# Scores at full height, out projections token-major, and x on a queue of its own, in a two-layer hybrid trunk

## The chip, the core and the metric

The kernel runs on one core of one Trainium2 chip. The metric is the device time of one execution in microseconds (us); the median of three executions of the kernel before is 894.36 us (894.18 to 894.96). One engine multiplies matrices (PE in the profile, with its weight loads as PEld), and beside it work VectorE (DVE), ScalarE (ACT), GpSimd (POOL) and SyncE (SP), each through its own queue of instructions in the order in which the program lists them. DMA transfers are issued from SP, ACT and POOL.

## The reference, cut to what matters

Two layers, a differential attention and a gated linear attention (GLA), over 256 tokens of width 2048, all in float32:

```python
def reference(x, ...):                       # x [1, 256, 2048]
    for i in range(2):
        h = _rmsnorm(x, norm_g[i])           # over the 2048 features
        y = _diff_attention(h, ...) if i == 0 else _gla(h, ...)
        x = x + y
    return x

def _diff_attention(h, w_in, qk_g, lam_vecs, subln_g, w_out, rel_bias, layer_idx):
    q, k, v, g = jnp.split(h @ w_in, 4, axis=-1)       # 16 heads, two halves t of 64 each
    q = _rmsnorm(q.reshape(B, S, H, 2, d), qk_g[0]) * (d ** -0.5)
    k = _rmsnorm(k.reshape(B, S, H, 2, d), qk_g[1])
...
    s = jnp.einsum('bqhtd,bkhtd->bthqk', qblk, k) + bias   # blocks of 128 queries
    s = jnp.where(_chunk_mask(qpos, kpos), s, NEG_INF)     # queries 0..127 see keys 0..127 alone
    p = jax.nn.softmax(s, axis=-1)
    attn = p[:, 0] - lam * p[:, 1]
...
    return (o * jax.nn.silu(g)) @ w_out

def _gla(h, w_in, w_gate, gate_bias, out_g, w_out):
    q, k, v, g, lr = jnp.split(h @ w_in, ...)
...
    return (o * jax.nn.silu(g)) @ w_out
```

## The kernel before, in words

**Products in split float32.** A float32 operand is split exactly into a high and a low part of type float32r ("fp32r" in the rows), and a product is made of three: high by high, low by high, high by low. Weights come in 288 chunks of 512 KB (`weights`, L93 to L110): SP issues the load into `raw` (four buffers, L104), ACT copies the high part (`hi`, L105), DVE subtracts it (`lo`, L108). For the first eight chunks SP also loads a piece of x ahead of the weights (L103), and `prep_x` makes the parts of x times the norm's gain in `aT` (`split_x`: ACT L188, DVE L189).

**Projections.** `project` (L141) takes the next 512 columns token-major, 16 contraction tiles of 128 rows: for each tile and each half t of the tokens three products of 512 columns (L159 to L161) into one bank of `pj` per half, 96 products in all; or it takes 256 columns feature-major: for each tile and each 128 output features one product of 512 columns (the tokens' high and low parts side by side, L163) and one of 256 (L165), 64 in all. The input projections of layer 0 and the values and gates of layer 1 are token-major; both out projections (`for blk in range(8)`) and the keys and queries of layer 1 are feature-major.

**Layer 0.** x lies feature-major in `xT`. Its squares are summed feature by feature: ACT squares (L180), POOL adds them up in `acc` (L182, L184), and `token_scale` (L203) lets PE sum over the partitions with products of one column (`ps_r`, L208). `norm_qk` writes a head's query parts as [high; low] over the 128 rows and the key's high part twice, so that one full-height product (L329) takes two of the three partial products; the third, high query by low key (`kl`), has 64 rows (L333). Each head does this for two halves t and two query blocks, 256 keys wide each, although block 0 uses only its first 128 columns (L339). Transpositions (`pt_qk`, `pt_a`, `pt_y`) are float32 products with the identity. The out projection adds its two halves into `xT` on DVE (L461), splits the sum for layer 1 at once and adds up its squares.

**Order.** The program names engines, not places: a scheduler orders each engine's instructions when the kernel is built. `background` holds generators (attention, gates, GLA) of which `pump` puts a piece behind every few chunks.

## Time and profile before

| | before |
|---|---|
| median of 3 executions | 894.36 us |
| the profiled execution, first to last instruction | 894.6 us |
| PE busy | 881.3 us, 99% |
| DVE, ACT, POOL busy | 573.4, 469.1, 117.9 us |
| mean granted clock of PE | 0.995 |
| DMA | 162.36 MB, mean 181 GB/s |

A busy PE is a row of overlapping products: each row of a product lasts longer than the time until the next one starts, so what a product costs is read from start to start. The rows further down are of four views: the page's first part (busy time, share and count of each engine), the waits, the timeline (start, duration, engine, line, what is written from what, count, and the idle time before), and tables of stretches or of groups of instructions.

### The profile page before, as it was taken

What the parts mean: (1) busy time and instruction counts of PE and PEld (TensorE: products, weight loads), DVE (VectorE), ACT (ScalarE), POOL (GpSimd) and SP (SyncE); (2) the same over time, 40 slices, a digit from 0 to 9 for tenths busy, and PEclk for the clock granted to TensorE, in tenths of its full rate; (3) what the DMA queues carried; (4) which work ended last, traced back from release to release, by engine and by line L of the source; (5) the groups of instructions that cost most, each with busy time, mean ns of one, the idle gap of its engine ahead of it and who ended that gap; (6) DMA issues with size and microseconds to landing.
All of it is one profiled execution on the core that took longest, in us unless ns stands there. A gap on an engine that the chain in (4) does not pass through costs nothing.

```text
span 894.6 us, 11955 instructions
## 1 busy us (share of the span) xinstructions
PE 881.3 (99%) x4388; PEld 733.7 (82%) x4388; DVE 573.4 (64%) x880; ACT 469.1 (52%) x727; POOL 117.9 (13%) x154
## 2 busy tenths in 40 slices
PE   7899999999999999999999999999999999999998
PEld 4688888888878878888888888888888888888886
DVE  5776576677668667565777758945555556555553
ACT  6556566656656655544544448643444444444331
POOL 5421012122012210100411121310000000000000
PEclk9899999999999999999999999999999999999999
DMA  7775555556555554555655545555465556656761
GB/s 268 240 226 183 181 171 186 186 176 198 179 161 169 170 158 150 175 183 183 206 186 190 188 146 176 173 191 172 159 181 172 178 175 186 183 180 194 223 213 46
DMA packets 47995, 162.36 MB, mean 181 GB/s; under 512 B 6048, under 2 KB 8624, under 8 KB 47936
## 3 DMA queue, kind: packets, MB, share of 16 engines
q1 hardware_dynamic: 43200, 153.11, 54.1%
q0 software_dynamic: 2288, 6.38, 2.4%
q10 hardware_dynamic: 2448, 2.11, 0.7%
q8 instruction: 34, 0.56, 0.3%
q14 instruction: 25, 0.20, 0.1%
HBM read 159.46 MB, written 5.27 MB: 184 GB/s over the span
## 4 chain that ended last, share of the span: by engine, by line
PE 96%; DVE 1%; DMA 1%; issue 1%; SPq 0%; ACT 0%; DVEq 0%
PE pj L163 20%; PE pj L159 19%; PE pj L161 19%; PE pj L160 19%; PE pj L165 10%; PE ps_s L329 1%; PE ps_s L333 1%; DMA raw<-in_aw 1%; PE ps_o L614 1%; PE ps_at L600 1%; PE pt_qk L298 1%; PE pt_y L410 1%; PE pt_a L363 1%; DVE aT L189 1%; PE ps_lr L511 0%
## 5 line engine op out<-in xcount | busy, mean ns | idle before, releaser
L108 DVE TENSOR_TENSOR lo<-raw,hi 128x1024 fp32r<-128x1024 f32 (+1 forms) x290 | 354.0, 1222 | 215.8 <-ACT hi L105 212.4
L105 ACT ACTIVATE hi<-raw 128x1024 fp32r<-128x1024 f32 (+1 forms) x290 | 304.8, 1052 | 316.4 <-PE pj L160 169.5
L159 PE MATMUL pj<-hi,aT 128*128 128x512 f32 x768 | 304.8, 397 | 2.2 <-ACT hi L105 2.2
L161 PE MATMUL pj<-lo,aT 128*128 128x512 f32 x768 | 300.5, 394 | 5.3 <-DVE lo L108 5.2
L160 PE MATMUL pj<-hi,aT 128*128 128x512 f32 x768 | 301.9, 393 | 0.5 <-DVE aT L189 0.5
L163 PE MATMUL pj<-y,hi 128*128 128x512 f32 x512 | 179.8, 397 | 0.0
L161 PEld LDWEIGHTS pj<-lo,aT 128*128 128x128 f32 x768 | 144.4, 189 | 37.1 <-DVE lo L108 7.0
L159 PEld LDWEIGHTS pj<-hi,aT 128*128 128x128 f32 x768 | 144.9, 189 | 34.3 <-ACT hi L105 3.5
L160 PEld LDWEIGHTS pj<-hi,aT 128*128 128x128 f32 x768 | 145.0, 189 | 29.4 <-DVE aT L189 0.9
L165 PE MATMUL pj<-y,lo 128*128 128x256 f32 x512 | 143.0, 280 | 0.0
L163 PEld LDWEIGHTS pj<-y,hi 128*128 128x128 f32 x512 | 96.1, 188 | 23.0
L165 PEld LDWEIGHTS pj<-y,lo 128*128 128x128 f32 x512 | 96.4, 188 | 0.2
L163 PE MATMUL pj<-aT,hi 128*128 128x512 f32 x256 | 90.5, 398 | 0.0
L165 PE MATMUL pj<-aT,lo 128*128 128x256 f32 x256 | 71.9, 281 | 0.0
L163 PEld LDWEIGHTS pj<-aT,hi 128*128 128x128 f32 x256 | 48.1, 188 | 11.5
L165 PEld LDWEIGHTS pj<-aT,lo 128*128 128x128 f32 x256 | 48.3, 189 | 0.0
L200 POOL TENSOR_TENSOR rq<-ms,mhalf 128x8 f32<-128x8 f32 x16 | 29.7, 1864 | 24.8 <-DVE ms L288 24.8
L184 POOL TENSOR_TENSOR acc<-acc,sq 128x512 f32<-128x512 f32 x14 | 20.8, 1482 | 67.0 <-ACT sq L180 66.8
L189 DVE SCALAR_TENSOR_TENSOR aT<-xT,ng_sb,aT 128x256 fp32r<-128x256 f32 x32 | 27.9, 906 | 2.6 <-ACT aT L188 2.6
L634 POOL TENSOR_TENSOR kq<-kq,rb 128x256 f32<-128x256 f32 x16 | 17.5, 1099 | 67.5 <-DVE kq L632 62.3
L337 DVE CUSTOM_DVE_ANT_0 s<-ps_s,tb 128x256 f32<-128x256 f32 x32 | 13.5, 422 | 19.1 <-PE ps_s L333 19.1
L320 POOL DMA_DIRECT2D tb<-skew_d x16 | 9.1, 572 | 124.9 <-DVE nm L339 85.3
(166 smaller groups left out, 633.8 us busy)
## 6 DMA issues: line engine op xcount, KB each, us to landing
raw<-in_aw SPq DMA_DIRECT2D x126, 512.0 KB, 3.6
raw<-in_bwvg SPq DMA_DIRECT2D x64, 512.0 KB, 3.5
raw<-in_awo SPq DMA_DIRECT2D x32, 512.0 KB, 4.4
raw<-in_bwkq SPq DMA_DIRECT2D x32, 512.0 KB, 4.1
raw<-in_bwo SPq DMA_DIRECT2D x32, 512.0 KB, 4.4
skew_d<-bias_d POOLq DMA_DIRECT2D x8, 384.0 KB, 5.6
tb<-skew_d POOLq DMA_DIRECT2D x16, 128.0 KB, 2.8
out_dram<-ot ACTq DMA_DIRECT2D x16, 128.0 KB, 4.2
```

What stands on the lines that cost most here:

```text
L105: nc.scalar.activation(hi[:, ks, :], raw[:, ks, :], AF.Copy)
L108: nc.vector.tensor_tensor(out=lo[:, ks, :], in0=raw[:, ks, :], in1=hi[:, ks, :].bitcast(F32), op=ALU.subtract)
L159: nc.tensor.matmul(banks[t], lhsT=xh, rhs=hi[:, kk, :], start=first, stop=False)
L160: nc.tensor.matmul(banks[t], lhsT=xl, rhs=hi[:, kk, :], start=False, stop=False)
L161: nc.tensor.matmul(banks[t], lhsT=xh, rhs=lo[:, kk, :], start=False, stop=last)
L163: nc.tensor.matmul(banks[t], lhsT=hi[:, kk, sl], rhs=lhs[k].rearrange("p a s -> p (a s)"), start=first, stop=False, skip_group_check=True)
L165: nc.tensor.matmul(banks[t][:, 0:S], lhsT=lo[:, kk, sl], rhs=lhs[k][:, 0, :], start=False, stop=last, skip_group_check=True)
L184: nc.gpsimd.tensor_tensor(out=acc, in0=acc, in1=sq, op=ALU.add)
L189: nc.vector.scalar_tensor_tensor(out=dst[k][:, 1, :], in0=xT[:, k, :], scalar=g, in1=dst[k][:, 0, :].bitcast(F32), op0=ALU.mult, op1=ALU.s ...
L200: nc.gpsimd.tensor_tensor(out=dst, in0=src, in1=mhalf[:, 0:n], op=ALU.pow)
L337: nc.vector.tensor_tensor_reduce(out=s[:, t, 0:256], in0=ps[:, 0:256], in1=tb, scale=1.0, scalar=BIG, op0=ALU.add, op1=ALU.min, accum_out= ...
L634: nc.gpsimd.tensor_tensor(out=dst, in0=dst, in1=rb, op=ALU.mult)
```

## The change

1. **Scores.** `kl` is two standing tiles with a half for each t, whose other 64 rows POOL sets to zero at the start. The third partial product becomes a full-height one with the same weights as the first. Query block 0 takes only keys 0 to 127, so that half of a head's eight products are 128 columns wide. The order is now by block, then by t.
2. **Out projections.** Both run token-major, four blocks of 512 columns. The residual x lies token-major in `xk`, loaded from a second copy of x (`xs`) by four SP transfers in the first projection block. DVE adds one bank at a time. The squares are taken token-major by ACT with an accumulated sum (`ssq`), no longer by POOL and PE. For layer 1, PE transposes the new x (`pt_x`, 32 transpositions in 8 groups), and ACT and DVE split it from PSUM.
3. **The start.** The feature-major x comes in five pieces, issued by ACT; DVE instead of ACT copies the high part of the first chunk. The last out block ends its last chunk bank by bank, and its output leaves in halves on two queues.

```diff
-                nc.sync.dma_start(xT[:, kx, :], xt[:, kx, :])
-            nc.sync.dma_start(raw[:, ks, :], src[:, ks, :])
-            nc.scalar.activation(hi[:, ks, :], raw[:, ks, :], AF.Copy)
+                high_x(pos[0] * CK + k, step)
+            if pos[0] == 0:
+                nc.vector.tensor_copy(out=hi[:, ks, :], in_=raw[:, ks, :])
+            else:
+                nc.scalar.activation(hi[:, ks, :], raw[:, ks, :], AF.Copy)
             if pos[0] < NCK:
-                prep_x(pos[0] * CK + k, step)
+                low_x(pos[0] * CK + k, step)
...
+            if tail and c == n - 1:
+                for t in range(2):
+                    for kk in range(ck):
+                        xh, xl = (lhs[c * ck + kk][:, i, t * P:(t + 1) * P] for i in range(2))
...
-    acc = const.tile([P, 2, S], F32, name="acc")
-    def square_sum(src, pool, first):
-        sq = pool.tile([P, 2, S], F32, tag="sq", name="sq", bufs=2 if pool is ta else 1)
-        nc.scalar.activation(sq, src, AF.Square)
-        if first:
-            nc.gpsimd.tensor_copy(acc, sq)
-        else:
-            nc.gpsimd.tensor_tensor(out=acc, in0=acc, in1=sq, op=ALU.add)
-    def split_x(layer, dst, k):
-        g = ng_sb[:, layer, k:k + 1]
-        nc.scalar.activation(dst[k][:, 0, :], xT[:, k, :], AF.Copy, scale=g)
-        nc.vector.scalar_tensor_tensor(out=dst[k][:, 1, :], in0=xT[:, k, :], scalar=g,
-                                       in1=dst[k][:, 0, :].bitcast(F32), op0=ALU.mult, op1=ALU.subtract)
+    xT = big.tile([P, KT, S], F32, tag="y1", name="xT")
+    for a, b in ((0, 1), (1, 2), (2, 4), (4, 8), (8, 16)):
+        nc.scalar.dma_start(xT[:, a:b, :], xt[:, a:b, :])
+    def high_x(k, n):
+        for i in range(k, k + n):
+            nc.scalar.activation(aT[i][:, 0, :], xT[:, i, :], AF.Copy, scale=ng_sb[:, 0, i:i + 1])
+    def low_x(k, n):
+        for i in range(k, k + n):
+            nc.vector.scalar_tensor_tensor(out=aT[i][:, 1, :], in0=xT[:, i, :], scalar=ng_sb[:, 0, i:i + 1],
+                                           in1=aT[i][:, 0, :].bitcast(F32), op0=ALU.mult, op1=ALU.subtract)
+    ssq = const.tile([P, 2, 4], F32, name="ssq")
+    def square_sum(blk, pool):
+        for t in range(2):
+            jk = pool.tile([P, NB], F32, tag="sq", name="sq", bufs=2 if pool is ta else 1)
+            nc.scalar.activation(jk, xk[:, t, blk * NB:(blk + 1) * NB], AF.Square, accum_out=ssq[:, t, blk:blk + 1])
...
-        tot = acc[:, 0, :]
-        nc.vector.tensor_tensor(out=tot, in0=acc[:, 0, :], in1=acc[:, 1, :], op=ALU.add)
-        ps = bank(ptr, "ps_r")
-        for t in range(2):
-            nc.tensor.matmul(ps[:, t:t + 1], lhsT=tot[:, t * P:(t + 1) * P], rhs=ones[:, 0:1],
-                             start=True, stop=True)
         ms = small.tile([P, 2], F32, tag="ms2", name="ms2")
-        nc.vector.tensor_scalar(out=ms, in0=ps[:, 0:2], scalar1=1.0 / D, scalar2=EPS, op0=ALU.mult, op1=ALU.add)
+        nc.vector.tensor_reduce(out=ms, in_=ssq, axis=AX.X, op=ALU.add)
+        nc.vector.tensor_scalar(out=ms, in0=ms, scalar1=1.0 / D, scalar2=EPS, op0=ALU.mult, op1=ALU.add)
...
+    kls = []
+    for i in range(2):
+        kl = ta.tile([P, 2, 4, S], F32R, name=f"kl{i}", bufs=1)
+        for t in range(2):
+            nc.gpsimd.memset(kl[64 - t * 64:128 - t * 64, t].bitcast(F32), 0.0)
+        kls.append(kl)
+    def load_x(c):
         if c >= NCK // 2:
-            for i in (2 * c - NCK, 2 * c - NCK + 1):
-                square_sum(xT[:, i * CK:(i + 1) * CK, :], ta, i == 0)
+            blk = c - NCK // 2
+            cols = slice(blk * NB, (blk + 1) * NB)
+            nc.sync.dma_start(xk[:, :, cols], xs[:, :, cols])
...
-                    nc.vector.tensor_tensor(out=kl[own, :, toks], in0=ptv[own], in1=dst[own].bitcast(F32),
+                    nc.vector.tensor_tensor(out=kl[own, u, :, toks], in0=ptv[own], in1=dst[own].bitcast(F32),
...
-            for qb, c0 in ((1, 0), (0, 256)):
-                qs = [qk[:, t * 4 + h, qb * P:(qb + 1) * P] for t in range(2)]
+            for qb, c0, n in ((1, 0, 256), (0, 256, 128)):
                 for t in range(2):
-                    nc.tensor.matmul(pss[t][:, c0:c0 + S], lhsT=qs[t], rhs=qk[:, 8 + t * 4 + h, :],
+                    q = qk[:, t * 4 + h, qb * P:(qb + 1) * P]
+                    nc.tensor.matmul(pss[t][:, c0:c0 + n], lhsT=q, rhs=qk[:, 8 + t * 4 + h, 0:n],
                                      start=True, stop=False)
-                for t in range(2):
-                    rows = slice(t * 64, (t + 1) * 64)
-                    nc.tensor.matmul(pss[t][:, c0:c0 + S], lhsT=qs[t][rows], rhs=kl[rows, h, :],
-                                     start=False, stop=True)
+                    nc.tensor.matmul(pss[t][:, c0:c0 + n], lhsT=q, rhs=kl[:, t, h, 0:n], start=False, stop=True)
...
-        b = project(aT, True, steps=4 if hg else 0, before=sum_x if hg == 0 else None)
+        b = project(aT, True, steps=4 if hg else 0, before=load_x if hg == 0 else None)
         if hg == 0:
+            for i in range(4):
+                square_sum(i, ta)
+            r1, r1h = token_scale("r1")
             setup_a()
-            r1, r1h = token_scale("r1")
         qk = big.tile([P, KT, S], F32R, tag="y0" if hg % 2 == 0 else "y1", name="qk")
-        kl = ta.tile([P, 4, S], F32R, tag="kl", name="kl")
+        kl = kls[hg % 2]
...
-    for blk in range(8):
-        b = project(yT, False)
-        for j in range(2):
-            k = blk * 2 + j
-            for i in range(2):
-                nc.vector.tensor_tensor(out=xT[:, k, :], in0=b[j][:, i * S:(i + 1) * S], in1=xT[:, k, :], op=ALU.add)
-            split_x(1, bT, k)
-        square_sum(xT[:, blk * 2:blk * 2 + 2, :], tb_, blk == 0)
-    r2, r2h = token_scale("r2")
+    def transpose_x(blk):
+        square_sum(blk, tb_)
+        yield
+        for half in range(2):
+            pt = bank(ptr, "pt_x")
+            for j in range(2):
+                k = blk * 4 + half * 2 + j
+                for t in range(2):
+                    nc.tensor.transpose(pt[:, (j * 2 + t) * P:(j * 2 + t + 1) * P], xk[:, t, k * P:(k + 1) * P], ident)
+            for j in range(2):
+                k = blk * 4 + half * 2 + j
+                g = ng_sb[:, 1, k:k + 1]
+                p = pt[:, j * S:(j + 1) * S]
+                nc.scalar.activation(bT[k][:, 0, :], p, AF.Copy, scale=g)
+                nc.vector.scalar_tensor_tensor(out=bT[k][:, 1, :], in0=p, scalar=g,
+                                               in1=bT[k][:, 0, :].bitcast(F32), op0=ALU.mult, op1=ALU.subtract)
+            yield
+    for blk in range(4):
+        b = project(yT, True, steps=4)
+        cols = slice(blk * NB, (blk + 1) * NB)
+        for t in range(2):
+            nc.vector.tensor_tensor(out=xk[:, t, cols], in0=b[t], in1=xk[:, t, cols], op=ALU.add)
+        background.append(transpose_x(blk))
...
-    background.append(first())
     for h in range(BH):
-        b = project(bT, False, steps=3)
+        b = project(bT, False, steps=3 if h else 0, before=None if h else lambda c: pump((0, 2, 1, 0)[c]))
         if h == 0:
-            drain()
+            r2, r2h = scale_row()
...
-    for blk in range(8):
-        b = project(zT, False)
-        for j in range(2):
-            k = blk * 2 + j
-            ot = gp.tile([P, S], F32, tag="th", name="ot")
-            nc.vector.tensor_tensor(out=ot, in0=b[j][:, 0:S], in1=xT[:, k, :], op=ALU.add)
-            nc.vector.tensor_tensor(out=ot, in0=b[j][:, S:2 * S], in1=ot, op=ALU.add)
-            nc.scalar.dma_start(out[:, k, :], ot)
+    for blk in range(4):
+        b = project(zT, True, tail=blk == 3)
+        for t in range(2):
+            ot = gp.tile([P, NB], F32, tag="th", name="ot")
+            for half in range(2 if blk == 3 else 1):
+                n = NB // 2 if blk == 3 else NB
+                part = slice(half * n, (half + 1) * n)
+                cols = slice(blk * NB + half * n, blk * NB + (half + 1) * n)
+                nc.vector.tensor_tensor(out=ot[:, part], in0=b[t][:, part], in1=xk[:, t, cols], op=ALU.add)
+                (nc.sync if half else nc.scalar).dma_start(out[:, t, cols], ot[:, part])
...
-        "awo": blocks(a["a_w_out"][0], S),
+        "awo": blocks(a["a_w_out"][0], NB),
```

How this moves instructions is shown at two places, the start and the scores. ACT's queue at the start, the kernel before, from the first gains on; `aT` is the scaled x, `sq` the squares, `hi` the high parts of weights:

```order
L188 ACTIVATE aT<-xT,ng_sb 128x256 x2
L180 ACTIVATE sq<-xT 128x512
L105 ACTIVATE hi<-raw 128x1024
L188 ACTIVATE aT<-xT,ng_sb 128x256 x2
L180 ACTIVATE sq<-xT 128x512
L188 ACTIVATE aT<-xT,ng_sb 128x256 x2
L180 ACTIVATE sq<-xT 128x512
L105 ACTIVATE hi<-raw 128x1024
L188 ACTIVATE aT<-xT,ng_sb 128x256 x2
L180 ACTIVATE sq<-xT 128x512
L105 ACTIVATE hi<-raw 128x1024 x6
```

The same queue in the changed kernel, where `xk` is the token-major x:

```order
L108 ACTIVATE hi<-raw 128x1024
L196 ACTIVATE aT<-xT,ng_sb 128x256 x4
L108 ACTIVATE hi<-raw 128x1024
L196 ACTIVATE aT<-xT,ng_sb 128x256 x8
L108 ACTIVATE hi<-raw 128x1024
L209 ACTIVATE sq,ssq<-xk 128x512 x5
L273 ACTIVATE nb<-ps_b 16x384
L209 ACTIVATE sq,ssq<-xk 128x512 x3
L108 ACTIVATE hi<-raw 128x1024
L285 ACTIVATE le<-ls 128x2
L108 ACTIVATE hi<-raw 128x1024 x5
```

All eight squares now stand between the high parts of the fifth and the sixth chunk of weights, and they read `xk`. SP's queue at the start, the kernel before, where `raw` are the weights:

```order
L103 DMA xT<-in_xt 128x512 x2
L104 DMA raw<-in_aw 128x1024
L103 DMA xT<-in_xt 128x512
L104 DMA raw<-in_aw 128x1024 x122
L104 DMA raw<-in_awo 128x1024 x32
```

The same queue in the changed kernel:

```order
L102 DMA raw<-in_aw 128x512 x4
L102 DMA raw<-in_aw 128x1024 x3
L249 DMA xk<-in_xs 128x2x512 x4
L102 DMA raw<-in_aw 128x1024 x123
L102 DMA raw<-in_awo 128x1024 x32
```

The four loads of `xk` stand behind five chunks of weights (the first two in halves) and ahead of the sixth. PE's queue around the scores of a head, the kernel before:

```order
L161 MATMUL pj<-lo,aT 128x512
L329 MATMUL ps_s<-qk 128x256 x2
L333 MATMUL ps_s<-kl,qk 128x256 x2
L329 MATMUL ps_s<-qk 128x256 x2
L333 MATMUL ps_s<-kl,qk 128x256 x2
```

The same place in the changed kernel:

```order
L349 MATMUL ps_s<-qk 128x256
L351 MATMUL ps_s<-kl_120,qk 128x256
L349 MATMUL ps_s<-qk 128x256
L351 MATMUL ps_s<-kl_120,qk 128x256
L349 MATMUL ps_s<-qk 128x128
L351 MATMUL ps_s<-kl_120,qk 128x128
L349 MATMUL ps_s<-qk 128x128
L351 MATMUL ps_s<-kl_120,qk 128x128
```

The eight products of a head still stand together between two products of the projection; where pairs over two t took turns, now each L349 is followed by the L351 of the same t.

## Rows read from the trace of the kernel before

**Rows 1.** The page's first part: busy time, share and count of PE.

```profile
PE 881.3 (99%) x4388; PEld 733.7 (82%) x4388; DVE 573.4 (64%) x880; ACT 469.1 (52%) x727; POOL 117.9 (13%) x154
```

**Rows 2.** The waits of PE, whole program: total us, times, longest.

```profile
PE pj L161 <- DVE lo L108: 5.2, 3, 3.7
PE pj L159 <- ACT hi L105: 2.2, 3, 1.0
```

**Rows 3.** Timeline of PE around the scores of one head: start, duration, what.

```profile
92.49 0.40 PE L329 MATMUL ps_s<-qk 128*128 128x256 f32 x2
92.81 0.38 PE L333 MATMUL ps_s<-kl,qk 64*128 64x256 f32 x2
93.12 0.50 PE L329 MATMUL ps_s<-qk 128*128 128x256 f32 x2
93.56 0.38 PE L333 MATMUL ps_s<-kl,qk 64*128 64x256 f32 x2
...
94.67 0.40 PE L159 MATMUL pj<-hi,aT 128*128 128x512 f32 x1
```

**Rows 4.** Timeline of PE, token-major projection, from one product to the third after it.

```profile
410.00 0.39 PE L161 MATMUL pj<-lo,aT 128*128 128x512 f32 x1
...
410.68 0.39 PE L161 MATMUL pj<-lo,aT 128*128 128x512 f32 x1
```

**Rows 5.** Timeline of PE: four float32r products of full height, 256 columns.

```profile
534.44 0.63 PE L535 MATMUL ps_z<-lrs,wgs 128*128 128x256 f32 x4
534.91 0.28 PE L165 MATMUL pj<-aT,lo 128*128 128x256 f32 x1
```

**Rows 6.** Timeline of PE: float32 products of 128 columns, two passes each.

```profile
135.81 0.39 PE L372 MATMUL po<-v,atT 128*128 128x128 f32 x2
136.04 0.39 PE L373 MATMUL po<-v,atT 128*128 128x128 f32 x2
```

**Rows 7.** Timeline of PE, feature-major out projections: twelve pairs, then thirty-one.

```profile
441.07 0.40 PE L163 MATMUL pj<-y,hi 128*128 128x512 f32 x1
...
445.31 0.40 PE L163 MATMUL pj<-y,hi 128*128 128x512 f32 x1
...
879.20 0.39 PE L163 MATMUL pj<-y,hi 128*128 128x512 f32 x1
...
889.94 0.40 PE L163 MATMUL pj<-y,hi 128*128 128x512 f32 x1
```

**Rows 8.** Timeline of PE around a group of four transpositions.

```profile
403.83 0.60 PE L410 MATMUL pt_y<-ident,th 128*128 128x128 f32 x4
...
404.97 0.40 PE L159 MATMUL pj<-hi,aT 128*128 128x512 f32 x1
```

**Rows 9.** The chain of waits, the one-column products of a token scale.

```profile
520.96 0.34 PE ps_r L208 x4
```

**Rows 10.** Stretches: us, PE, PEld, DVE, ACT, POOL busy (count), PE clock, DMA share, GB/s.

```profile
5.10:27.30 22.20, 17.93 (x68) 11.74 (x66) 16.79 (x23) 16.48 (x32) 11.06 (x12) 1.00 0.81 277
27.30:31.40 4.10, 0.43 (x3) 0.04 (x1) 4.10 (x5) 2.57 (x3) 2.11 (x2) 0.80 0.60 203
31.40:37.00 5.60, 5.60 (x14) 4.42 (x15) 4.43 (x6) 0.77 (x1) 1.77 (x4) 0.54 0.74 212
37.00:41.20 4.20, 4.20 (x21) 3.46 (x20) 2.00 (x2) 1.35 (x2) 0.00 (x0) 1.00 0.99 366
```

**Rows 11.** ACT by form: count, busy us, mean ns; first two of 0:41.2.

```profile
L105 ACT ACTIVATE hi<-raw 128x1024 fp32r<-128x1024 f32 x9 | 9.2, 1049 | 8.5 <-DMA raw<-in_aw 8.4
L188 ACT ACTIVATE aT<-xT,ng_sb 128x256 fp32r<-128x256 f32 x16 | 7.4, 498 | 0.7 <-DMA ng_sb<-in_ng 0.5 <-DMA xT<-in_xt 0.2
...
L617 ACT ACTIVATE jkb<-ps_o 128x512 f32<-128x512 f32 x8 | 4.7, 588 | 2.3 <-PE ps_o L614 2.3
...
L617 ACT ACTIVATION_READ_ACCUMULATOR jkb<-ps_o 128x1 f32 x8 | 1.5, 192 | 0.0
```

**Rows 12.** Timeline of DVE: the last instructions of the program.

```profile
890.83 0.75 DVE L680 TENSOR_TENSOR ot<-pj,ot 128x256 f32<-128x256 f32 x2
```

More of the change, by code (lines that the diff above doesn't have):

```diff
@@ L80, in trunk_kernel @@
         nc.tensor.matmul(idle, lhsT=zero[:, 0:P], rhs=zero, start=True, stop=True)
-    xT = big.tile([P, KT, S], F32, name="xT")
+    xk = big.tile([P, 2, D], F32, name="xk")
     def operand(tags):
@@ L139, in drain, with project @@
             pump()
-    def project(lhs, token_major, steps=0, before=None):
+    def project(lhs, token_major, steps=0, before=None, tail=False):
         banks = [bank(pj, "pj"), bank(pj, "pj")]
@@ L166, in project @@
                                          start=False, stop=last, skip_group_check=True)
+            if tail and c == n - 1:
+                for t in range(2):
+                    for kk in range(ck):
+                        xh, xl = (lhs[c * ck + kk][:, i, t * P:(t + 1) * P] for i in range(2))
+                        nc.tensor.matmul(banks[t], lhsT=xh, rhs=hi[:, kk, :], start=False, stop=False)
+                        nc.tensor.matmul(banks[t], lhsT=xl, rhs=hi[:, kk, :], start=False, stop=False)
+                        nc.tensor.matmul(banks[t], lhsT=xh, rhs=lo[:, kk, :], start=False, stop=kk == ck - 1)
             want = (c + 1) * steps // n
@@ L220, in trunk_kernel @@
     ta = lay_a.enter_context(tc.tile_pool(name="ta", bufs=2))
-    def prep_x(k, n):
-        for i in range(k, k + n):
-            split_x(0, aT, i)
-    def sum_x(c):
+    kls = []
[5 more added lines that the diff above has]
+    def load_x(c):
         if c >= NCK // 2:
-            for i in (2 * c - NCK, 2 * c - NCK + 1):
-                square_sum(xT[:, i * CK:(i + 1) * CK, :], ta, i == 0)
+            blk = c - NCK // 2
+            cols = slice(blk * NB, (blk + 1) * NB)
+            nc.sync.dma_start(xk[:, :, cols], xs[:, :, cols])
     relb_sb = const.tile([32, AH], F32, name="relb_sb")
```

16 lines of the change are left out of this document (9 added, 7 removed).

## The prediction

> **What bounds the kernel now.** The first part of the page shows PE busy for 99% of the span [rows 1]. Read alone, that says only that products overlap, so the waits come next: over the whole program PE waits 5.2 us for low parts of weights and 2.2 us for high parts, three times each [rows 2], and by the timeline all of it lies in the first 32 us. Behind the start PE waits for nothing, so each microsecond taken from PE's row there shortens the program, and nothing done for DVE, ACT or POOL does, as long as none of them becomes late. Durations in PE's rows overlap; I read prices from start to start.
>
> **The change part by part.** The sum is made against the profiled execution's 894.6 us.
>
> *Scores.* The eight products of a head start at 92.49, and the fourth projection product behind them starts at 94.67 [rows 3]. Between lie 2.18 us, less three projection products of 0.227 (three take 0.68 [rows 4]): a head costs 1.50 us. The eight products have 256 columns each, and full-height float32r products of 256 columns, each with weights of its own, run at 0.47 us for four, 0.1175 apiece [rows 5]; eight would be 0.94. The missing 0.56 us is the turn between full and half height: the two half-height products at 92.81 hand over only at 93.12, and the next full-height pair at 93.12 takes 0.44 until 93.56 [rows 3]. The change makes all eight full height, with the same rows of queries as weights. Four keep 256 columns. The other four have 128, and no float32r product of 128 columns is in this trace. From below: half of 0.1175, if columns alone count, 0.059. From above: a float32 product of 128 columns, which is run as two passes, takes 0.23 (135.81 to 136.04 [rows 6]). I take 0.1175, no gain from fewer columns, since the weights are as large as before and rows 5 is the nearest in type. So a head costs 0.94, and 16 heads save 16 x 0.56 = 9.0 us. With 0.059 a head costs 0.71 and the saving is 12.7; with 0.23 it costs 1.39 and the saving is 1.8.
>
> A rule of the Trainium skill speaks against this edit: page "TensorEngine Tiling (Array Packing)", section "Theoretical Speedup", gives up to twofold speed for a contraction of 64 rows or fewer. By it a pair of half-height products would cost one full one, a head before would be 0.71 us, and the edit would lose 0.23 x 16 = 3.8 us. The measured 1.50 of rows 3 leaves that no chance; the same page says that a change of tiling mode drains the engine, which fits the late turns. On width, page "TensorE: Matmul & The Clock Gate", section "Back-to-back issue gap", gives N / 2.4 + 2.5 ns, some 56 ns at 128 columns; no run here shows it yet.
>
> *Out projections.* Columns are the same: per contraction tile and 512 features, four pairs of 512 and 256 before, six products of 512 after. The pace is not. Twelve pairs take 4.24 us in the first out projection, 0.353 a pair, and thirty-one take 10.74 in the second, 0.3465 [rows 7]; 256 pairs each make 90.4 + 88.7 = 179.1 us. Token-major, 256 groups of three at 0.68 [rows 4] make 174.1: 5.0 us saved. From the other side, if token-major took the slower column pace of rows 7, 256 x 0.7066 = 180.9, a loss of 1.8; I take 5.0, since rows 4 are the same instructions on the same shapes. Weights still come in chunks of 512 KB with one ACT copy and one DVE subtraction each, so their supply per product of PE does not change.
>
> *Transpositions of x.* They are new on PE. A group of four starts at 403.83, and the fourth product behind it at 404.97: 1.14 - 0.68 = 0.46 us [rows 8]. Eight groups cost 3.7, and one is torn in two by the order, about 0.1 more: 3.8 us. ACT and DVE split x from PSUM beside PE; the last block's groups stand behind the first products of layer 1, which need them only for the last quarter of their contraction.
>
> *Token scale.* Four records of one column, 0.34 us in the chain [rows 9], go in each layer; with some 0.05 for the turn, 0.8 us saved.
>
> *The start.* Of the first 41 us, 22.2 from 5.1 on hold only 17.9 of overlapping products, then PE stands for 4.1, and from 31.4 to 37.0 it runs at a granted clock of 0.54 [rows 10], near the lower of its two levels of 1.2 and 2.4 GHz, after having stood. 5.6 x (1 - 0.54) = 2.6 us is the price of that. DVE was at work in all of the 4.1 us: its splits of x ran beside POOL's additions. Counted along the timeline, the first block's 96 products are out at 41.2; unhindered from 5.1 on they would be at 26.9. The change takes POOL's additions away but moves the squares: ACT's queue holds eight of them between the high parts of chunks five and six, and they read `xk`, which SP loads behind five chunks of weights. Queued behind them on ACT is every later high part, and PE waits for that. Bytes first: x 2.1 MB, five chunks 2.6, xk 2.1, together 6.8 MB; at 277 GB/s [rows 10] that is 24.5 us from about 2.5 on, so 27; at 366 GB/s, 21. Then ACT: the last piece of x is in at some 16.5 (4.2 MB at 300, between those two rates; ACT's five issues ahead lie within that time), eight gains of 0.46 (they overlap a little; 0.498 each [rows 11]) to 20.2, the high part of chunk five 1.05 to 21.3, eight squares of 0.588 + 0.192 [rows 11] and a small copy of 0.5 to 28.0, the sixth high part to 29.1. PE is done with chunk five at 24.0 and stands for five microseconds, longer than before, so I charge the 2.6 us of the clock again. Three chunks of 36 products, 8.2 us, end at 37.4, with the clock at 40.0: 1.2 us saved. At best, with a fast xk and no fall of the clock, 36: 5 saved. At worst xk comes at 203 GB/s, the lowest rate in rows 10: 6.8 MB take 33.5, two squares and the high part follow at 38.6, then 8.2 + 2.6 make 49.4: 8.2 lost.
>
> That x has a queue of its own I count at nothing: with one queue the DMA engines already reached a share of 0.81 to 0.99 [rows 10].
>
> *The end.* The last two additions of 0.75 us [rows 12] become one second addition of about 0.36, and the halves leave on two queues: 0.4 us saved.
>
> *At nothing:* the zeros of `kl` on POOL lie ahead of all scores; larger squares with an accumulated sum cost ACT time that it has (52% busy [rows 1]); the shift of the phase in which the feature-major products of layer 1 run (0.353 or 0.3465 a pair, 256 pairs) may give or take 1.7 us.
>
> **The sum.** -9.0 - 5.0 + 3.8 - 0.8 - 1.2 - 0.4 = -12.6, so 882.0 us as profiled. The profiled execution lies 0.24 above the median; the forecast for the median is 881.8.
>
> **The rivals.**
> A. *Narrow products are slow.* A float32r product of 128 columns takes the two passes of rows 6, 0.23. For it: those are the only products of that width. Against it: they are float32, not float32r. Scores then save 1.8, and the time is 889.0.
> B. *Only columns count.* 0.059 for 128 columns: 12.7 saved, 878.1. For it: 256 columns of rows 5 cost about half of 512 in rows 4. Against it: the load of 128 columns of weights under each product, which does not shrink. The gap cited above would give this case.
> C. *Full height does not free the products.* The 0.22 of a full-height product in the second pair of rows 3 may belong to the scores' own weights and banks, not to the half-height neighbours. At 0.216 a product, 1.73 a head, the loss of 3.6 us eats all that the rest saves; above that the kernel is slower, and at 0.25 it takes 898.8. Against it: rows 5, where weights also change with each product.
> D. *ACT stands for xk.* The late case of the start: 891.2, and with narrow products slow too it would be no gain at all. Against it: DMA reached 366 GB/s when it was asked.
>
> **How the numbers follow.** The forecast, 877 to 886, has a chance of 0.61; A 0.20, B 0.10, C 0.04, D 0.05. The 80% range reaches from 874 (B with a good start) to 890 (A with a start that saves nothing); out of it are C, D and the far ends of A and B. No difference is what a measurement of this kernel can't tell, some 0.2%, or 1.8 us: faster means below 892.6. Faster 0.93, the same 0.03 (D with part of A, C near its point), slower 0.04 (C beyond it).
>
> **What would show it.** Score groups of about 0.94 us from start to start would show the first term right, 1.4 would show A, 0.7 B, 1.8 or more C. Out projections should show three products per 0.68 us and `pt_x` groups of 0.46. At the start, PE should stand between chunks five and six while ACT squares, and the first block should end at about 40; a wait of ACT for `in_xs` would show D. If PE waits for anything behind 45 us, an engine that I took for idle has become late, and the forecast is wrong by that wait.

## The result, and the profile after

The changed kernel takes 880.42 us (median of four executions, 879.58 to 880.88) beside 894.66 us of the kernel before on the same chip: a ratio of 0.984, 95% interval 0.982 to 0.985. That is 14.2 us less, where 12.6 was forecast.

One correction first. The results give the span of each execution beside its time, and the time is 1.8 to 2.0 us longer (after: 878.9 and 880.88). So the profiled execution of before, with a span of 894.6, was itself slower than the median by some 2 us, an estimate; the prediction took its span for a time. The forecast for the median stood, since the sum is a difference, but of the 15.8 us between the two profiles about 1.5 is that one execution's. It lies in the start by what the other runs show, since behind product 97 the kernels that share their code take the same time within 0.2 us in each stretch. Between two median executions the start therefore gains some 1.7 us, an estimate, where the table has 3.26.

The stages of the two profiled executions, read from the timeline from product to product ("product 97" is the 97th of `pj`, the first of the second block):

| stretch, us | before | after | change | predicted |
|---|---|---|---|---|
| first instruction to product 97 | 41.17 | 37.91 | -3.26 | -1.2 |
| to the first product of the first out projection | 379.25 | 368.73 | -10.52 | -9.4 (scores, one token scale) |
| first out projection | 91.30 | 90.90 | -0.40 | +0.1 for this and the next row |
| layer 1 to the second out projection | 288.72 | 289.16 | +0.44 | |
| second out projection, to its last product | 89.73 | 87.77 | -1.96 | -1.7 |
| from the last product to the end | 4.48 | 4.41 | -0.07 | -0.4 |

The page's first part, which answers [rows 1], and the waits of PE, which answer [rows 2]:

```profile
PE 867.8 (99%) x4156; PEld 721.6 (82%) x4156; DVE 548.6 (62%) x836; ACT 468.6 (53%) x741; POOL 99.4 (11%) x142
```

```profile
PE pj L164 <- ACT hi L108: 2.4, 1, 2.4
PE pj L164 <- ACT aT L196: 2.3, 3, 1.6
PE ps_idle L81 <- DVE zero L78: 1.2, 1, 1.2
PE pj L165 <- DVE aT L200: 1.0, 2, 0.5
```

PE has the same share of a shorter span. No wait for low parts of weights is left, and by the timeline all of these waits still lie in the first 28 us. A head's scores in the timeline of PE (start, duration), which answer [rows 3]:

```profile
163.89 0.28 PE L349 MATMUL ps_s<-qk 128*128 128x256 f32 x1
164.00 0.28 PE L351 MATMUL ps_s<-kl,qk 128*128 128x256 f32 x1
...
164.36 0.22 PE L349 MATMUL ps_s<-qk 128*128 128x128 f32 x1
164.41 0.28 PE L351 MATMUL ps_s<-kl,qk 128*128 128x128 f32 x1
164.53 0.28 PE L349 MATMUL ps_s<-qk 128*128 128x128 f32 x1
164.64 0.28 PE L351 MATMUL ps_s<-kl,qk 128*128 128x128 f32 x1
164.75 0.45 PE L164 MATMUL pj<-hi,aT 128*128 128x512 f32 x1
165.03 0.39 PE L165 MATMUL pj<-hi,aT 128*128 128x512 f32 x1
```

From start to start: 0.11 to 0.12 at 256 columns; at 128 columns 0.057 for the first (0.05 by the rounded rows) and 0.11 for the rest; and the projection product behind them takes 0.28 where 0.227 is usual. A head costs 0.93 us in all.

A group of four transpositions with what follows (answers [rows 8]: 1.14 to the fourth product, less 0.68, is 0.46), and three products of an out projection (answers [rows 7], at the 0.68 of [rows 4]):

```profile
440.24 0.60 PE L484 MATMUL pt_x<-ident,xk 128*128 128x128 f32 x4
...
441.38 0.40 PE L164 MATMUL pj<-hi,y 128*128 128x512 f32 x1
```

```profile
410.04 0.39 PE L164 MATMUL pj<-hi,y 128*128 128x512 f32 x1
...
410.72 0.39 PE L164 MATMUL pj<-hi,y 128*128 128x512 f32 x1
```

The start in stretches (columns as in [rows 10], which it answers): the clock falls later and less, and in the middle stretch the transfers nearly stop, since the buffers of weights wait for ACT.

```profile
5.80:27.70 21.90, 16.40 (x63) 10.69 (x63) 12.75 (x30) 16.49 (x40) 4.20 (x10) 1.00 0.96 365
27.70:30.10 2.40, 2.34 (x7) 1.62 (x8) 2.40 (x5) 2.40 (x4) 1.38 (x3) 0.79 0.16 49
30.10:37.91 7.81, 7.81 (x30) 6.30 (x30) 2.81 (x4) 1.53 (x2) 0.06 (x1) 0.85 0.94 303
```

### The profile page after: what moved, and what is told of

Its sections match the earlier page's. It is cut to its first block, busy times and chain, and to the rows that moved or that the text cites. A ratio compares the mean times of both kernels' runs of the same rounds, so it can differ in the third digit from the quotient of the medians.

```text
span 878.9 us, 11444 instructions
## 1 busy us (share of the span) xinstructions
PE 867.8 (99%) x4156; PEld 721.6 (82%) x4156; DVE 548.6 (62%) x836; ACT 468.6 (53%) x741; POOL 99.4 (11%) x142
## 4 chain that ended last, share of the span: by engine, by line
PE 96%; ACT 1%; DMA 1%; DVE 0%; issue 0%; DVEq 0%
PE pj L166 26%; PE pj L164 26%; PE pj L165 26%; PE pj L168 7%; PE pj L170 3%; DMA raw<-in_aw 1%; PE ps_o L651 1%; PE ps_at L637 1%; PE ps_s L351 1%; PE pt_qk L318 1%; PE pt_y L427 1%; PE ps_s L349 1%; PE pt_a L380 1%; ACT aT L196 1%; ACT hi L108 0%; ACT sq L209 0%
## 5 line engine op out<-in xcount | busy, mean ns | idle before, releaser
L164 PE MATMUL pj<-hi,y 128*128 128x512 f32 x252 | 98.9, 392 | 0.0
L166 PE MATMUL pj<-lo,y 128*128 128x512 f32 x252 | 98.3, 390 | 0.0
L165 PE MATMUL pj<-hi,y 128*128 128x512 f32 x252 | 98.1, 389 | 0.0
L166 PEld LDWEIGHTS pj<-lo,y 128*128 128x128 f32 x252 | 47.3, 188 | 9.8
L165 PEld LDWEIGHTS pj<-hi,y 128*128 128x128 f32 x252 | 47.4, 188 | 9.6
L164 PEld LDWEIGHTS pj<-hi,y 128*128 128x128 f32 x252 | 47.3, 188 | 9.6
L219 POOL TENSOR_TENSOR f<-zz,mhalf 128x2 f32<-128x2 f32 x16 | 11.2, 705 | 100.5 <-DVE zz L398 100.4
```

The source lines that it names most:

```text
L164: nc.tensor.matmul(banks[t], lhsT=xh, rhs=hi[:, kk, :], start=first, stop=False)
L165: nc.tensor.matmul(banks[t], lhsT=xl, rhs=hi[:, kk, :], start=False, stop=False)
L166: nc.tensor.matmul(banks[t], lhsT=xh, rhs=lo[:, kk, :], start=False, stop=last)
L219: nc.gpsimd.tensor_tensor(out=dst, in0=src, in1=mhalf[:, 0:n], op=ALU.pow)
```

## Experiments on the scores

**The score part alone, and all but it.** In the first kernel the kernel before gets the new `kl`, its zeros and the new loop; in the second the kernel after gets the old ones back. The core of the second edit:

```diff
-            for qb, c0, n in ((1, 0, 256), (0, 256, 128)):
+            for qb, c0 in ((1, 0), (0, 256)):
...
+                for t in range(2):
+                    rows = slice(t * 64, (t + 1) * 64)
+                    nc.tensor.matmul(pss[t][:, c0:c0 + S], lhsT=qs[t][rows], rhs=kl[rows, h, :],
+                                     start=False, stop=True)
```

> The kernel before, with the score part of the change alone: key low parts padded with zeros to full height, the second query block 128 columns wide. Theory of the prediction, corrected by the trace after (0.92 us a head where 1.50 stood): 16 x 0.58 = 9.3 us less than before, so about 885.4; the start, both out projections and their pace stay as before. Rival, columns alone count: the gain in the trace after was helped by something else and a head costs 1.2 here, so 4.8 us less, about 889.9. Rival, the page's twofold speed for 64 rows: 3.8 us more, 898.5. The zeros on GpSimd lie ahead of its additions of squares; if they delay the start, the first block ends later than 41.2.

> The kernel after, with the score part undone: low parts of the keys at half height, both query blocks 256 wide. Theory: a head costs 1.50 again instead of 0.92, 16 x 0.58 = 9.3 more than after, 889.7, ratio to before 0.994. If the score part explains less than the layer's measured 10.5 us of gain, the rest stays here. Rival (twofold speed for 64 rows): 876.6, faster than after.

The kernel with the score part undone takes 889.38 us (ratio 0.994, 0.993 to 0.995), as expected, and its stretch from product 97 to the out projection is 378.83 against 368.73: the score part is worth 10.1 us. The score part alone takes 880.53 (0.984, 0.983 to 0.985), where 885.4 was expected. Its scores' stretch is 369.21, 10.0 less than before, so that part is as large as it should be. The other 4.9 us lie at the start: product 97 comes at 36.27 instead of 41.17, although nothing there was meant to change. PE still stands for the same low part, 3.55 us instead of 3.67, but the stand ends at 27.31 instead of 31.36:

```profile
27.31 1.09 PE L161 MATMUL pj<-lo,aT 128*128 128x512 f32 x2 [3.55 <-DVE lo L108]
```

So some 4.0 us of the gain lie ahead of the stand and the rest behind it, where the clock falls for a shorter time. GpSimd's zero fills now stand ahead of its additions of squares, which fall elsewhere beside DVE. That this is the cause was not tried by itself, and DVE's splits of x are hardly shorter for it, 794 ns in the mean against 859; the cause stays open. The stretches, columns as in [rows 10]:

```profile
27.00:31.00 4.00, 3.69 (x9) 2.92 (x10) 4.00 (x7) 3.25 (x5) 3.03 (x1) 0.57 0.58 156
31.00:36.27 5.27, 5.27 (x25) 4.34 (x24) 4.23 (x4) 2.15 (x3) 2.88 (x4) 1.00 0.99 308
```

So a change of total time by one edit does not give that edit's price here; the stretch does.

**Fewer turns, and no narrow products.** The first kernel has half-height products as before, but four full ones and then four half ones in each head; the second is the kernel after with 256 columns in both blocks.

```diff
+            for qb, c0 in blocks:
+                for t in range(2):
+                    nc.tensor.matmul(pss[t][:, c0:c0 + S], lhsT=qk[:, t * 4 + h, qb * P:(qb + 1) * P],
...
+            for qb, c0 in blocks:
+                for t in range(2):
+                    rows = slice(t * 64, (t + 1) * 64)
...
```

```diff
-            for qb, c0, n in ((1, 0, 256), (0, 256, 128)):
+            for qb, c0, n in ((1, 0, 256), (0, 256, 256)):
```

> The same half-height products, but four full-height products first and then four of half height, so that a head turns from one height to the other twice instead of four times. Theory T, the missing time lies in the turns, each about 0.58 / 4 = 0.145 us: half of the loss is gone, 16 x 0.29 = 4.6 less than the kernel with four turns, about 885.0. Rival S, half-height products are slow whatever stands beside them: no difference, 889.7. Rival P, two half-height products of different rows run side by side once they stand together: four of them in 0.23 us, a head at about 0.47 + 0.23 + 0.29, so 888.5 - 7.4 = 882.

> The kernel after with 256 columns in both query blocks, as before the change. Theory W, a product of 128 columns costs as much as one of 256 since the weights behind it have to be loaded (0.112 measured for three of four, 0.057 for one): only that one loses, 16 x 0.07 = 1.1 more, 881.5, a head at 0.94 to 0.99. Rival B, columns count: four products of 0.0575 more in each head, 16 x 0.23 = 3.7 more, 884.1.

Two turns instead of four: the stretch is 372.15, 6.7 less than with four, and the time 882.43. Fifteen heads cost 1.115 each (timeline of PE; the rows stand for four products each), and one, in which the scheduler mixed the order, 1.615:

```profile
162.81 0.63 PE L343 MATMUL ps_s<-qk 128*128 128x256 f32 x4
163.37 0.50 PE L348 MATMUL ps_s<-kl,qk 64*128 64x256 f32 x4
163.80 0.50 PE L164 MATMUL pj<-hi,aT 128*128 128x512 f32 x1
```

```profile
163.59 0.28 PE L348 MATMUL ps_s<-kl,qk 64*128 64x256 f32 x2
```

Four half-height products take 0.43 here, and four full ones 0.47 [rows 5]: once they stand together they are not slow, which ends rival S. The size lies between the other two: theory T had 4.6 us for the sixteen heads and rival P 7.4, and the stretch shows 6.7. What tells them apart is the last row, from a timeline cut so that it shows the second pair alone. The first pair starts at 163.37 and the second at 163.59, so two half-height products take 0.22 together, not the 0.12 by which P has four in 0.23, and P's mechanism falls although its time, 882, came nearest. The kernel before gives a third point. In 14 heads it turns four times, for 1.503 us; in two heads the scheduler alternates one full product with one half one, and they turn six times (timeline of before):

```profile
328.46 0.28 PE L329 MATMUL ps_s<-qk 128*128 128x256 f32 x1
328.67 0.38 PE L333 MATMUL ps_s<-kl,qk 64*128 64x256 f32 x1
328.98 0.39 PE L329 MATMUL ps_s<-qk 128*128 128x256 f32 x1
329.29 0.38 PE L333 MATMUL ps_s<-kl,qk 64*128 64x256 f32 x1
329.61 0.50 PE L329 MATMUL ps_s<-qk 128*128 128x256 f32 x2
```

Those two cost 2.01. So no turn, two, four and six turns cost 0.93, 1.12, 1.50 and 2.01: about 0.1 us for each of the first two, 0.19 for each of the next two and 0.25 for each of the last two. The last step is not one of turns alone, since it also parts a pair: a half-height product by itself hands over after 0.31 (328.67 to 328.98), as a pair does (92.81 to 93.12 [rows 3]). The missing time lies in the turns, as theory T has it, but its equal price of 0.145 does not hold.

Wide products change next to nothing: the stretch is 368.83 against 368.73, a head 0.933 against 0.926, so even the 1.1 us that theory W gave them did not come. The 1.3 us by which this kernel is faster (879.13) lie at the start (product 97 at 36.82), where it runs the same instructions in the same order as the kernel after: they are no effect of the edit. Half the columns bring 0.1 us in the whole program, since what is saved at 164.36 above is paid back at 164.75. This speaks for the weights' load as the floor: 0.11 us for 128 columns of weights, whatever stands in front of them. The Trainium skill, page "TensorE: Matmul & The Clock Gate", section "LDWEIGHTS (loading the stationary operand)", gives P / 1.2 ns for P columns of weights, 107 ns at 128 by estimate; the 0.11 of this trace agrees.

## Experiments on the start

| kernel | product 97 at, us | time, us | ratio to before, interval |
|---|---|---|---|
| before | 41.17 | 894.7 to 895.8 | |
| before, no squares | 30.82 | 885.60 | 0.989, 0.988 to 0.990 |
| before, no additions | 31.78 | 886.34 | 0.990, 0.988 to 0.991 |
| after | 37.91 | 880.42 | 0.984, 0.982 to 0.985 |
| after, no squares | 34.20 | 877.07 | 0.980, 0.978 to 0.981 |
| after, xk late | 35.04 | 879.32 | 0.982, 0.981 to 0.984 |
| after, x on SP | 32.51 | 875.53 | 0.978, 0.977 to 0.979 |
| after, x on SP, xk late | 30.52 | 879.64 | 0.983, 0.981 to 0.984 |
| after, x on SP, xk a little earlier | 31.04 | 879.21 | 0.983, 0.982 to 0.984 |

Product 97 is read from one profiled execution, whose time may lie up to 1.4 us off the median (before, by the estimate above, 2). The kernel after and the one with wide products, alike up to there, reach it at 37.91 and 36.82. So a difference of about 1 us in the first column says nothing.

**What held up the start before.** Squares left out altogether, and then only GpSimd's additions of them:

```diff
-            for i in (2 * c - NCK, 2 * c - NCK + 1):
-                square_sum(xT[:, i * CK:(i + 1) * CK, :], ta, i == 0)
+            if c == NCK // 2:
+                nc.vector.memset(acc, 8.0)
```

```diff
-        else:
+        elif pool is not ta:
             nc.gpsimd.tensor_tensor(out=acc, in0=acc, in1=sq, op=ALU.add)
```

> The kernel before without the squares of x in layer 0 and their additions on GpSimd: the sums are set to a constant, so this part is left out. Theory G, GpSimd's additions stretch DVE's splits beside them (four splits took 5.67 us where 1.75 is their usual time): DVE's splits come down to 0.44 each all through the start, PE's wait of 3.7 us is gone, the 97th product starts at 34 to 36 instead of 41.2, and the time is 888 to 890. Rival, the start is bound by the transfers: the 97th product stays behind 39 and the time within 2 us of 894.7.

> The kernel before with its squares of layer 0 on ACT as they are, but without GpSimd's additions of them: only the first square reaches the sum, the others are left out of it. Theory G, the additions beside DVE's splits are the cause of the late start: as in the kernel without squares (97th product at 30.8, 885.6), 31 to 33, 885.5 to 888. Rival A, ACT's time for the squares is the cause: the 97th product stays at 38 or later, 892 or more. Between them lies the share of each.

Both came out on theory G's side, the first further than it forecast (30.82 instead of 34 to 36, 885.60 instead of 888 to 890). The additions alone are worth 9.4 us at product 97, and as much in the time (886.34 beside 895.76 of the kernel before on the same chip); the 1.0 us more without ACT's squares is no more than two profiles of the same start differ by. DVE's sixteen splits of x in the first 41.2 us (groups by form: count, busy, mean ns), before and without the additions:

```profile
L189 DVE SCALAR_TENSOR_TENSOR aT<-xT,ng_sb,aT 128x256 fp32r<-128x256 f32 x16 | 13.2, 859 | 2.6 <-ACT aT L188 2.6
```

```profile
L189 DVE SCALAR_TENSOR_TENSOR aT<-xT,ng_sb,aT 128x256 fp32r<-128x256 f32 x16 | 7.1, 479 | 4.1 <-ACT aT L188 4.0
```

The same sixteen instructions take 6.1 us less. Without the additions PE also keeps a granted clock of 1.00 from 5.1 us to product 97, so the 2.6 us that the prediction reckons for the clock in [rows 10] are part of the 9.4. The Trainium skill, page "GPSIMD Engine Reference", section "1. Specifications", says that GpSimd shares its SBUF interfaces with VectorE and contends with DVE instructions that have two SBUF inputs, as this one does; 859 against 479 ns agrees.

**What holds it up after.** Squares left out; the loads of `xk` and the squares moved behind the first block; x on SP's queue.

```diff
-            for i in range(4):
-                square_sum(i, ta)
+            nc.vector.memset(ssq, 100.0)
```

```diff
+            nc.vector.tensor_copy(out=xk[:, 0, blk * NB:blk * NB + 1], in_=lo[:, 0, 0:1].bitcast(F32))
             nc.sync.dma_start(xk[:, :, cols], xs[:, :, cols])
...
+            b0 = b
+            background.append(squares())
+            b = project(aT, True, steps=4, after=load_x)
```

```diff
+            if pos[0] < NCK:
+                kx = slice(pos[0] * CK + k, pos[0] * CK + k + step)
+                nc.sync.dma_start(xT[:, kx, :], xt[:, kx, :])
...
-    for a, b in ((0, 1), (1, 2), (2, 4), (4, 8), (8, 16)):
-        nc.scalar.dma_start(xT[:, a:b, :], xt[:, a:b, :])
```

> The kernel after without the eight squares of x in layer 0: their sums are set to a constant, so this part of the computation is left out; xk is still loaded at the same place. Theory S, the squares in ACT's queue between the high parts of chunks five and six are what the rest of the start waits for: in the kernel after, PE loses 4.6 us between its 60th and 97th product; without the squares the 97th starts at 33 to 34 instead of 37.9, and the time is about 876. Rival X, the bytes of xk hold up the chunks behind them: the sixth high part then waits for its chunk and the 97th product still starts at 36.5 to 38, 879 to 880.5.

> The kernel after with the four loads of xk and the squares moved behind the first block: each load waits, by a one-column copy, for the low part of one of chunks eight to eleven, the squares follow on ACT among the high parts of the second block, and the queries' norm comes behind the second block's products. Nothing is left out. By theory S and by X alike the start must gain: no squares ahead of chunk six and 2.1 MB less ahead of chunk five, the 97th product at 31 to 34. By how much it beats the kernel without squares is the price of the bytes. Expected 874 to 877, if the norm, now 20 us later, keeps no product waiting; if it does, PE waits behind 50 us for pj or for a transposition of qk and the gain of 4 us is lost.

> The kernel after with x loaded again as before, on SP's queue, a piece ahead of each weight chunk, instead of five pieces on ACT's own queue. The prediction counted the queue at nothing, since one queue already kept the DMA engines at a share of 0.81 to 0.99: 880.4 within 1 us, the 97th product at 37 to 39. Rival, one queue halves what x gets: x's last piece lands some 4 us later, the gains of the last eight tiles and all behind them too, 884.

Theory S holds: without the squares PE loses nothing behind chunk five and product 97 starts at 34.20. ACT in the kernel after, the two high parts with the squares between them:

```profile
20.37 1.04 ACT L108 ACTIVATE hi<-raw 128x1024 fp32r<-128x1024 f32 x1
21.32 0.61 ACT L209 ACTIVATE sq<-xk 128x512 f32<-128x512 f32 x1
...
26.59 1.04 ACT L108 ACTIVATE hi<-raw 128x1024 fp32r<-128x1024 f32 x1
```

The kernel without squares still loads `xk` at the same place, so rival X falls, and moving the bytes of `xk` away as well brings no more (35.04). The kernel with `xk` late missed its own expectation, 31 to 34 and 874 to 877: PE stands 2.15 us for the gains of chunk three, behind which the granted clock is 0.70 up to 20.25, where the kernel after keeps 1.00. Its executions also lie farther apart than the others', from 878.03, the profiled one, to 881.97; what makes the slower ones slow no run shows. The third kernel overturned my own expectation, and its rival too: the queue that was counted at nothing costs 5.4 us at product 97 and 4.9 us in the time. Some 1.7 us of that is the clock, an estimate from the stretches of the kernel after (2.40 x 0.21 + 7.81 x 0.15): with x on SP it keeps 1.00. The third chunk's high part on ACT, in the kernel after and with x on SP:

```profile
13.56 1.06 ACT L108 ACTIVATE hi<-raw 128x1024 fp32r<-128x1024 f32 x1 [3.11 <-DMA raw<-in_aw]
```

```profile
11.70 1.06 ACT L111 ACTIVATE hi<-raw 128x1024 fp32r<-128x1024 f32 x1 [0.78 <-DMA raw<-in_aw]
```

The transfers were not slower; they carried other bytes. The queues of the kernel after from 6 to 14 us (q10 is ACT's, with x; q1 is SP's, with the weights and xk):

```profile
DMA packets 927, 3.06 MB, mean 383 GB/s; under 512 B 207, under 2 KB 215, under 8 KB 801
q10 hardware_dynamic: 410, 1.77, 58.3%
q1 hardware_dynamic: 349, 1.12, 37.0%
```

Two queues share the engines, and x, of which PE needs an eighth with each chunk, takes most of them while ACT waits for the third chunk. With x on SP the same eight microseconds move only 336 GB/s, but in the order of need. The Trainium skill, page "DMA: Bandwidth & Descriptors", section "Queues, rings and completion order", says that an engine goes round the queues that have work packet by packet; the profile's 410 and 349 packets, not far from equal turns, agree. With this order of arrival the scheduler also spreads ACT's gains and squares over its gaps, which the runs do not separate. But with the squares late in both, the queue still makes 35.04 against 30.52, so 4.5 us, the clock's share included, are not the squares'.

**Both moves together.** They looked additive, and were not:

> Both of the helpful moves in the kernel after, nothing left out: x on SP's queue a piece ahead of each weight chunk (875.5 alone), and xk with its squares behind the first block (879.3 alone, its 97th product at 35.0 instead of 37.9). In the kernel with x on SP, PE still loses 1.9 us between its 72nd and 84th product, where squares stand ahead of the seventh high part; if they are its cause, the 97th product starts at 30.5 to 31 instead of 32.5, and the time is 873.5 to 874. Rival: what is left of the start is the order in which the bytes come (1.7 lost by product 36, 2.7 by 60), and the squares only took time that ACT had; then nothing moves, 875 to 876.

> The kernel with x on SP's queue and xk moved, with xk's loads let go earlier: two behind the low part of chunk six, two behind that of chunk seven, into the stretch of 24 to 28 us in which the transfers stood at 120 to 207 GB/s, and all eight squares in a row on ACT behind the twelfth high part. Nothing is left out. Theory L, with the loads behind chunks eight to eleven the last piece of xk landed at 48.1 and the token scale came 5.5 us too late for the queries' transpositions at 52.4: now xk lands by 34, the squares end by 39, the transpositions wait for nothing, the 97th product starts at 30.5 to 31.5, and the time is 873.5 to 874.5, below all others. Rival, eight squares in a row on ACT starve the products of high parts between 35 and 45 us: PE waits there for hi, as long as the squares take beyond the lead of four chunks, 1 to 3 us, and the time is 875 to 877.

In the first, product 97 starts at 30.52 as expected, and the time is 879.64: 4.1 us slower than x on SP alone. PE now waits for the queries' transpositions behind the second block (timeline), and ACT had waited for the last piece of `xk`:

```profile
57.94 1.08 PE L322 MATMUL pt_qk<-ident,qn 128*128 128x128 f32 x4 [5.49 <-DVE qn L317]
```

```profile
48.11 0.63 ACT L212 ACTIVATE sq<-xk 128x512 f32<-128x512 f32 x1 [2.74 <-DMA xk<-in_xs]
```

In the second, the loads go earlier (two behind chunk six, two behind seven), and the rival came true, with a larger loss than its 875 to 877: the squares, the first of which starts only at 35.03 when `xk` has landed, keep ACT from the twelfth chunk's high part, and PE stands 3.6 us for it:

```profile
42.93 0.80 PE L169 MATMUL pj<-hi,aT 128*128 128x512 f32 x1 [3.56 <-ACT hi L111]
```

Both kernels win 1.5 to 2.0 us in the first block, little more than two like profiles differ by, and from product 97 to the out projection they take 376.31 and 374.09 us where x on SP alone takes 368.69. The stands are not all of that: behind them the granted clock falls, to 0.75 from 58 to 66 us in the first kernel and 0.78 from 43 to 50 in the second. With x on ACT's queue the late squares displaced nothing in the profiled execution (368.75), perhaps since its whole start was later; with the early start both places that were tried displace something that PE needs, while at the start itself the squares lie beside work that waits for bytes. The best version run is therefore x on SP alone, 875.53 us: 4.9 us below the changed kernel.

## Experiment on the out projections

The second out projection feature-major again, eight blocks of pairs:

```diff
-    for blk in range(4):
-        b = project(zT, True, tail=blk == 3)
+    for blk in range(8):
+        b = project(zT, False)
...
```

> The kernel after with its second out projection feature-major again: eight blocks of 256 columns, pairs of 512 and 256 columns, each bank added in two halves, one output transfer a block. The residual and the places in the output are left token-major, so that the output does not mean the reference's, while the work is that of the kernel before. Theory, the pace of pairs is what was saved: 88.7 + 1.0 for the end of the last block (89.73 was measured before) against 87.77, so 2.0 us more than after, 882.4. Rival, the pace comes from the phase in which pairs run (0.353 or 0.3465) and token-major gains nothing by itself: 880.4.

The stretch is 89.73, to the hundredth that of the kernel before, against 87.77: the pace of the pairs, 2.0 us, is the theory's. The time of 884.11 (0.987, 0.986 to 0.989) is 3.7 above the kernel after. The other 1.3 us lie behind the last product, 5.67 to the end against 4.41, where this kernel adds each bank in two steps and sends one transfer; what in it takes longer than the 4.48 of the kernel before was not tried.

## Why the prediction came out as it did

**What bounds the kernel.** Right. PE stays at 99%, no wait of the changed kernel stands behind the start, and the stretches from the first out projection on come out alike within 0.01 us in kernels that share their code (91.30 or 90.90, 288.72 or 289.16).

**Scores: mechanism right, size short.** 10.1 instead of 9.0. A head after costs 0.926 (0.94 was taken), but the price before was read from one head, 1.50, and multiplied by 16. Fourteen heads fit: 14 x 0.577 = 8.1. Two with six turns give 2 x 1.08 = 2.2. The term should have been read over all groups. Taking 0.1175 for narrow products came out, and the wide kernel speaks for the reason given, the load of the weights. The formula of 56 ns that the prediction cites from the Trainium skill (page "TensorE: Matmul & The Clock Gate", section "Back-to-back issue gap") is there the gap of a product alone, with the note that it counts too little for narrow products in a stream with weight loads. The 0.11 us here agrees with the note. Rivals A (1.4 us a head), B (0.7) and C (1.8) fall.

**Out projections and transpositions.** Right: 0.68 a triple, 0.46 a group of four. First projection, transpositions and the token scale of layer 1 together make +0.04 against +0.1. The second projection saves 1.96 against 1.65: the pairs of before took 89.73 in all where 0.3465 gave 88.7, since the thirty-one from which it was read ran faster than the whole, and the triples took 87.77 where 0.68 gave 87.0.

**Token scale.** Right in size: the stretch of layer 0 is 369.21 with the one-column products and 368.73 without, 0.5, and with the old scores 379.25 and 378.83, 0.4.

**The start: sign right, working wrong.** Two steps failed. "That x has a queue of its own I count at nothing" failed: the DMA engines' share was full, as [rows 10] say, but which bytes fill it is what counts, and the queue costs 5.4 at product 97. And the removal of GpSimd's additions was named but not priced: I saw that DVE's splits ran beside them and then costed only the new chain of ACT. It is worth 9.4. The two nearly cancel: 9.4 - 5.4 leaves 4.0, beside the 3.3 measured; the difference is not split up by these runs. That 1.2 stood close to the 3.3, and to the 1.7 between medians, is luck. The chain of ACT itself held roughly. The last gain ended at 20.46 (20.2 forecast). The sixth high part ended at 27.63 instead of 29.1, because the reading of a sum overlaps the next square (0.61 from square to square, not 0.78). PE stood 2.4 us for it instead of five, since it was done with chunk five only at 25.3 instead of 24.0. The clock fell for less long than before. ACT never waited for `xk`, so rival D is out.

**The tail.** 0.07 instead of 0.4: the step that failed is the one second addition. Both halves of the last bank are still added behind it, 0.75 us, and that bank's last product now has 512 columns, 0.39 instead of 0.28:

```profile
874.47 0.39 PE L178 MATMUL pj<-lo,y 128*128 128x512 f32 x1
874.89 0.75 DVE L715 TENSOR_TENSOR ot<-pj,xk 128x256 f32<-128x256 f32 x2 [0.60 <-PE pj L178]
```

## What to carry to other kernels

Where an instruction changes how much of the array is used, count the turns and not the rows alone: here filling half an operand with zeros was cheaper than turning. A full DMA share says nothing on whether the bytes come in the order of need; a second queue for a stream that is consumed in step with another one takes its turn from it. And when a wait at the start is removed by moving work to a later place, look there first for what that work will displace.

## What the runs showed of the hardware that was not expected

- Two half-height products on different rows begin 3 ns apart, so they do run side by side, and yet a pair takes 0.22 us at 256 columns (163.37 to 163.59), nearly as long as two full-height ones (0.23). The up to twofold speed of the Trainium skill (page "TensorEngine Tiling (Array Packing)", section "Theoretical Speedup") is not to be had here for float32r, apart from the turns.
- A product of 128 columns among others with weights of their own costs what one of 256 does, 0.11 us; only the first of a row starts early, and the next wide product gives it back.
- GpSimd's elementwise additions stretched DVE's splits from 0.44 us to 1.4 us where they met (four took 5.67 us).
- With PE standing 1.03 and 1.25 us in two places, the kernel with x on SP kept a granted clock of 1.00 through the start. In the kernel after, with waits of 1.6 and 2.4 us, it was 0.79 and 0.85 behind the second, and with the score part alone 0.57 behind one of 3.55, near the lower of its two levels of 1.2 and 2.4 GHz. The length of a stand alone does not tell: with x on SP and `xk` a little earlier PE stood 2.14 us ahead of 13.27 and the clock kept 1.00.
